# Emitting evictions and selection steps by modelled engine clocks, with two count chains, and FFN tiles in other pools

## The chip, the cores and the metric

The kernel runs on one core of one Trainium2 chip. The metric is the device time of one execution in microseconds (us). The core has TensorE (PE, matmuls; PEld is its weight load), VectorE (DVE), ScalarE (ACT), GpSimd (POOL) and SyncE (SP, which only issues DMAs). Each engine has a stream of instructions of its own, in the order in which the program holds them.

## The reference

One encoder layer on 2048 tokens of width 1024, in float32. Cut to what matters here:

```python
proj = x @ w_in                     # q, latent k/v, index q, index w, index k, pool input, two gates
rel = relu(einsum('bqhd,bsd->bqhs', q_idx, k_idx) * idx_scale)
idx_score = einsum('bqh,bqhs->bqs', w_idx * head_w_scale, rel)     # masked to admissible chunks
_, sel = top_k(idx_score, 256)      # each query attends to its 256 best keys
attn = softmax(q . k_lat[sel] * attn_scale) @ v_lat[sel]           # 8 heads, shared latent key/value
branch_a = (attn @ w_uv) @ w_attn_branch
branch_b = pool(pool_in) @ w_pool_branch       # trailing means over 2, 4, 8, 16 frames minus the frame
mixed = (sigmoid(gate_a) * branch_a + sigmoid(gate_b) * branch_b) @ w_out
x = layer_norm(ALPHA * x + mixed)
h = causal_conv3(x @ w_ffn_up); ffn = (silu(gate) * val) @ w_ffn_down
x = layer_norm(ALPHA * x + ffn)
```

## The kernel before

Every float32 product is made of three matmuls on a high and a low part (`mm3`); a part is made by a copy on ACT (`hi`) and a subtraction on DVE or POOL (`lo`). The stages follow one another: the index projections (`proj_index`, four token groups g of 512 tokens, to about 200 us), then for each g the pool projections, the query projections and the gates (`proj_pool`, `proj_q`, `proj_gates`, to about 1110 us), the attention (to about 1690 us), the mixing (`mix_out`, to about 1975 us), the FFN's up-projection in two halves (`up`, to about 2850 us) and its down-projection (`down`).

From `proj_pool` of g = 0 to the end of `proj_gates` of g = 3 the instructions are held in the order in which the Python program emits them, on every engine (`manual_schedule`, L827). The generators of the projections yield after every six matmuls, and `turn` (L379) is called at each yield. It puts in steps of a background generator (`bg`): the index scores of a token group (`index_scores`, L861) and then the selection of the 256 best keys (`select`, L935), for the groups (0, 1), 2 and 3 of `GROUPS` in turn. The selection is a search over 32 bits: each bit counts, for each block of 128 queries, how many scores reach a threshold tile `F`, and `decide` (two small DVE instructions) makes the next `F`. Half of the blocks are counted on DVE, the others on ACT (Sign with an accumulated output), which waits for `F` from DVE. After the bits a mask is made per block (ACT Sign, a scan and other steps on DVE) and stored (`msk`).

How much background `turn` puts in is ruled by a model: `Paced` adds a modelled cost to a clock of each engine (`Clocks`), and `turn` goes on while the slower of DVE and ACT is under `SLACK` = 3 us ahead of PE and a credit lasts, which grows with 0.75 of PE's modelled time. Some costs of the model are a PE matmul of n columns at 0.002 + n/2400 us, a fixed 0.05 us on ACT (0.28 with accumulated output), 0.07 us on DVE, and a scan at 1.04 ns an element.

The evictions of the projections' results from PSUM (four one-bank tiles `p1`) are emitted at fixed places: in `proj_q` (L677) an ACT copy right after the matmuls of each 128 tokens; after four of them `rope` on DVE rotates the rows, and `store_q` (L701) transposes earlier rows on PE and copies them out on ACT. The pool windows run on POOL in steps (`lazy_step`); one call after a window's last addition `less` (L758) emits, in one go, a DVE subtraction into `m`, the ACT copy of its high part, which reads `m`, and the DVE low part. The sigmoid gates are emitted two turns later (`after`).

`load_q` (L1054) needs the mask of block b and drains the background until it is emitted; `end_selection` (L304), called before the attention's block 8, drains all that is left.

In the FFN's up-projection (a held order as well, planned in `plan_up`, L1511, by due times around a period of 19.04 us for each of 44 quads of seven products) SBUF tiles of 4 KB a partition come from two pools: `T` (`big`, 34 tiles) and `L` (`more`, 12 tiles). Input combinations p = 1 and 2 (`x_load` L1437, `x_split` L1447) lie in `L`, the other five in `T`, four tiles each; the weights' parts (`up_hi`) and the convolution's sums (`conv_first`) lie in `T`, the raw weights in `L`.

Of the kernel before, what the change touches and what calls it, by code (L numbers as in the profile page):

```python
# [9 lines left out]
F32 = mybir.dt.float32  # L10
# [38 lines left out]
SLACK = 3.0  # L49
NPRE = 2  # L50
PN = (1, 1, 1)
PG = (0,)
HD, HP = 3, 5
# [5 lines left out]
DG = 2  # L59
DQ = 0  # L60
MS = 'vector'
FIN = 1
# [9 lines left out]
PAUSE = "pause"  # L72
GRAIN = 1
RATE = 0.75
CAP = 1.5
SCAN = 1.04
# [8 lines left out]
class Clocks:  # L85
# [7 lines left out]
    def slowest(self):  # L93
        return max(self.dve, self.act)

    def backlog(self):
        return self.slowest() - self.pe


class Paced:  # L100
# [5 lines left out]
    def __getattr__(self, name):  # L106
# [135 lines left out]
class Kern:  # L242
    def __init__(self, ctx, tc, a, out):
        self.clocks = Clocks()
        self.tc, self.nc, self.a, self.out = tc, PacedCore(tc.nc, self.clocks), a, out
        self.stores, self.older, self.bg, self.late = [], [], [], []
        self.const = ctx.enter_context(tc.tile_pool(name="const", bufs=1))
# [16 lines left out]
        self.credit = self.seen = 0.0  # L264
# [21 lines left out]
    def PS1(self, shape=(P, 512)):  # L286
        return self.p1.tile(list(shape), F32, tag="p1", name=self._name("p1_"))
# [16 lines left out]
    def end_selection(self):  # L304

        while self.bg:
            drain(self.bg.pop(0)[1])
# [70 lines left out]

    def turn(self, step=None):  # L379
# [8 lines left out]
        pe, work = self.clocks.pe, self.clocks.work  # L388
        self.credit = min(self.credit + RATE * (pe - self.seen), CAP)
        self.seen = pe  # L390
        while self.bg and self.clocks.backlog() < SLACK and self.credit > 0:
            ready, gen = self.bg[0]
            if not ready():
                break
            before = dict(work)
            step = next(gen, "end")
            if step == "end":
                self.bg.pop(0)
            if step == PAUSE:
                break  # L400
            self.credit -= max(work["dve"] - before["dve"], work["act"] - before["act"])
# [275 lines left out]
    def proj_q(self, g):  # L677
# [1197 lines left out]
```

## Time and profile before

| what | value |
|---|---|
| median of 3 runs | 3349.55 us (3349.07 to 3350.21) |
| the profiled execution | 3349.93 us, span of its instructions 3348.2 us |
| PE busy | 3203.2 us, 96% of the span |
| DVE, ACT, POOL busy | 2114.3, 1644.9, 1324.2 us |

A busy time is the time in which the engine had at least one instruction under way. The waits name what ended an idle stretch. [...] All operations are recorded through one helper, so every instruction has line 135, and tiles are told apart by name: `p` is PSUM, `b` a tile of `T`, `l` of `L`, `m` of the pool `mid`, `i` a row of scores, `F` and `h` the thresholds and their steps.

### The profile page before, as it was taken

How to read it: one execution, taken by the hardware profiler on the slowest of the kernel's cores; microseconds unless marked ns; L12 is line 12 of the kernel's file. 1: busy time of each engine (PE TensorE's matmuls, PEld its weight loads, DVE VectorE, ACT ScalarE, POOL GpSimd, SP SyncE). 2: the span in 40 equal slices, each digit the busy share in tenths (PEclk: the TensorE clock that was granted, in tenths of full speed). 3: DMA queues.
4: the chain of work that ended last, by engine and by line, in shares of the span. 5: the costliest groups of instructions: out<-in, count | busy, mean ns of one | idle time of the engine just before them, and what ended most of it. 6: DMA issues, size and time to landing. Idle time of an engine off the chain costs nothing. (4 is left out here: it accounts for less than half of the span.)

```text
span 3348.2 us, 45033 instructions
## 1 busy us (share of the span) xinstructions
PE 3203.2 (96%) x16198; PEld 2711.3 (81%) x16198; DVE 2114.3 (63%) x3724; ACT 1644.9 (49%) x2720; POOL 1324.2 (40%) x1283
## 2 busy tenths in 40 slices
PE   8899989989989799999999999999999999999998
PEld 8898878888878578888878878888778888888887
DVE  5567677876778787777755775565655455643543
ACT  3456636754667566666621134444544444433431
POOL 3148410010010432111221157777667777644552
PEclk9999999999989899999999999999999999999999
DMA  8368944735545211000164762332422222655552
GB/s 318 120 233 283 350 160 151 289 137 178 211 177 179 91 62 37 30 31 16 31 209 157 271 218 82 113 126 95 157 76 90 93 82 92 219 167 175 192 178 85
DMA packets 260142, 499.12 MB, mean 149 GB/s; under 512 B 19210, under 2 KB 136910, under 8 KB 259918
## 3 DMA queue, kind: packets, MB, share of 16 engines
q1 hardware_dynamic: 231182, 461.64, 39.8%
q10 hardware_dynamic: 28736, 34.61, 2.9%
q8 instruction: 127, 2.08, 0.3%
q14 instruction: 97, 0.79, 0.1%
HBM read 349.21 MB, written 146.96 MB: 148 GB/s over the span
## 5 line engine op out<-in xcount | busy, mean ns | idle before, releaser
L135 PE MATMUL p<-b,b 128*128 128x512 f32 (+3 forms) x12480 | 2642.0, 368 | 97.2 <-ACT b L135 45.0
L135 PEld LDWEIGHTS p<-b,b 128*128 128x128 f32 x12480 | 2147.3, 191 | 467.6 <-ACT b L135 51.5
L135 ACT ACTIVATE b<-p 128x512 fp32r<-128x512 f32 (+12 forms) x610 | 373.0, 632 | 351.4 <-PE p L135 337.0
L135 POOL TENSOR_TENSOR b<-b,b 128x256 fp32r<-128x256 f32 (+3 forms) x302 | 441.5, 1467 | 234.0 <-ACT b L135 196.4
L135 ACT ACTIVATE b<-i,F 128x1408 bf16<-128x1408 f32 (+4 forms) x224 | 322.1, 1438 | 154.3 <-DVE F L135 112.4
L135 ACT ACTIVATE b<-b 128x1024 fp32r<-128x1024 f32 (+2 forms) x264 | 231.7, 909 | 316.5 <-DMA b<-h 164.1
L135 PE MATMUL p<-l,b 128*128 128x512 f32 x1440 | 349.2, 397 | 1.6 <-DVE b L135 1.6
L135 POOL TENSOR_SCALAR b<-b 128x256 fp32r<-128x256 f32 (+3 forms) x214 | 113.5, 533 | 570.5 <-ACT b L135 287.1
L135 PEld LDWEIGHTS p<-l,b 128*128 128x128 f32 x1440 | 270.7, 188 | 66.6 <-DVE b L135 2.4
L135 DVE TENSOR_SCALAR_CACHE_REDUCE b<-i,F 128x1152 bf16<-128x1152 f32 (+7 forms) x238 | 314.8, 1323 | 3.6
L135 DVE TENSOR_TENSOR b<-b 128x512 fp32r<-128x512 f32 (+1 forms) x104 | 159.5, 1543 | 231.4 <-ACT b L135 227.8
L135 DVE TENSOR_TENSOR b<-p,b 128x512 fp32r<-128x512 f32 (+2 forms) x330 | 254.3, 780 | 62.5 <-ACT b L135 57.5
L135 POOL TENSOR_TENSOR b<-m,b 128x512 fp32r<-128x512 f32 x176 | 236.4, 1366 | 96.8 <-ACT b L135 94.2
L135 ACT ACTIVATE b<-m 128x512 fp32r<-128x512 f32 x224 | 136.2, 626 | 259.3 <-POOL m L135 166.4
L135 DVE TENSOR_TENSOR p<-p,m 128x512 f32<-128x512 f32 x132 | 91.8, 695 | 252.2 <-PE p L135 252.0
L135 ACT ACTIVATE b<-p,cw 128x1024 f32<-128x1024 f32 x88 | 106.3, 1208 | 282.9 <-DVE p L135 282.9
L135 PE MATMUL p<-ident,b 128*128 128x128 f32 x1456 | 215.0, 275 | 22.1 <-ACT b L135 12.2
L135 POOL TENSOR_TENSOR b<-l,b 128x512 fp32r<-128x512 f32 x132 | 173.8, 1332 | 135.2 <-ACT b L135 135.1
L135 DVE SCALAR_TENSOR_TENSOR b<-p,cw,b 128x1023 f32<-128x1023 f32 (+1 forms) x132 | 169.0, 1281 | 88.6 <-ACT b L135 54.9
L135 PEld LDWEIGHTS p<-ident,b 128*128 128x128 f32 x1456 | 175.0, 141 | 57.1 <-ACT b L135 15.7
L135 DVE CUSTOM_DVE_ANT_0 b<-p,b 128x1024 f32<-128x1024 f32 (+7 forms) x192 | 174.4, 909 | 68.3 <-PE p L135 67.7
L135 DVE SCALAR_TENSOR_TENSOR i<-b,ws,i 128x768 f32<-128x768 f32 (+9 forms) x154 | 154.8, 1027 | 59.5 <-ACT b L135 57.8
(136 smaller groups left out, 2224.3 us busy)
## 6 DMA issues: line engine op xcount, KB each, us to landing
b<-wp SPq DMA_DIRECT2D x192, 512.0 KB, 6.6
l<-in_w_ffn_up_dram SPq DMA_DIRECT2D x88, 512.0 KB, 5.1
b<-in_w_ffn_down_dram SPq DMA_DIRECT2D x88, 512.0 KB, 4.4
wp<-b SPq DMA_DIRECT2D x64, 512.0 KB, 6.6
h<-b SPq DMA_DIRECT2D x44, 512.0 KB, 2.7
b<-h SPq DMA_DIRECT2D x88, 256.0 KB, 3.9
b<-in_w_in_dram SPq DMA_DIRECT2D x32, 512.0 KB, 7.4
xT<-b SPq DMA_DIRECT2D x32, 512.0 KB, 6.9
```

Source lines behind the costliest of these rows:

```text
L135: return f(*args, **kw)
```

## The change

The costs of the clocks' model are set anew, the credit goes, and `SLACK` becomes 2.0 us, for each engine by itself. A heap of due steps is added: `evict` emits an eviction at the first turn at which the modelled PE clock is 0.25 us past its last matmul, and a following stage at the time at which the model has the earlier engine done. No more than two evictions (three in `pool_map`) stay open when a new `p1` tile is taken. The steps of `less`, of the scores and of the masks are cut apart in the same way. The background becomes a list of tasks, each bound to some engines; a task may yield a time until which it is held, or WAIT. In `select` the counts on ACT are a task of their own (`signs`), beside the counts on DVE, and each count there is held until the model has its threshold ready. In the FFN, `x` tiles p = 1 and 2 move from `L` to `T`, and the parts A11 and S2 and the convolution's sums from `T` to `L`. No arithmetic is changed. The diff, cut (the steps left out are cut apart in the same manner as those shown):

```diff
 LEAD = 2.5
-SLACK = 3.0
...
-SCAN = 1.04
+SCAN = 2.2
 PIECE = 256
...
             if self._w == "pe":
-                self._c.pe += 0.109 if name == "transpose" else 0.002 + max(n, 64) / 2400.0
+                self._c.pe += 0.109 if name == "transpose" else max(0.106, 0.0134 + n / 2400.0)
             else:
                 rate = {"dve": 1.04, "act": 0.84, "pool": 2.2}[self._w]
-                fixed = 0.07
-                if self._w == "act":
-                    fixed = 0.28 if "accum_out" in kw else 0.05
-                if self._w == "dve" and name in ("tensor_scalar", "tensor_copy") and "accum_out" not in kw:
+                fixed = 0.17
+                if "accum_out" in kw:
+                    fixed = 0.47 if self._w == "act" else 0.29
+                elif self._w == "dve" and name in ("tensor_scalar", "tensor_copy"):
...
-    def PS1(self, shape=(P, 512)):
+    def PS1(self, shape=(P, 512), ahead=2):
+        while len(self.open) > ahead:
+            self.evict_step(self.open[0], True)
         return self.p1.tile(list(shape), F32, tag="p1", name=self._name("p1_"))
...
-        while self.bg:
-            drain(self.bg.pop(0)[1])
+        self.force(lambda: not (self.tasks or self.bg))
...
 
+    def when(self, time, f):
+
+        self.serial += 1
+        heapq.heappush(self.due, (time, self.serial, f))
+
+    def run_due(self, until=None):
+        while self.due and self.due[0][0] <= (self.clocks.pe if until is None else until):
+            heapq.heappop(self.due)[2]()
+
+    def evict(self, *stages):
+
+        e = list(stages)
+        self.open.append(e)
+        self.when(self.clocks.pe + 0.25, lambda: self.evict_step(e))
+
+    def evict_step(self, e, all=False):
+        while e:
+            engine, f = e.pop(0)
+            f()
+            if e and not all:
+                self.when(getattr(self.clocks, engine), lambda: self.evict_step(e))
+                return
+        self.open = [o for o in self.open if o is not e]
+
     def turn(self, step=None):
         for t in self.late:
...
             self.older, self.stores = self.stores, []
-        pe, work = self.clocks.pe, self.clocks.work
-        self.credit = min(self.credit + RATE * (pe - self.seen), CAP)
-        self.seen = pe
-        while self.bg and self.clocks.backlog() < SLACK and self.credit > 0:
-            ready, gen = self.bg[0]
-            if not ready():
-                break
-            before = dict(work)
-            step = next(gen, "end")
-            if step == "end":
-                self.bg.pop(0)
-            if step == PAUSE:
-                break
-            self.credit -= max(work["dve"] - before["dve"], work["act"] - before["act"])
+        self.run_due()
+        self.background()
+
+    def spawn(self, gen, *engines):
+        task = {"gen": gen, "engines": engines, "hold": 0.0}
+        self.tasks.append(task)
+        return task
+
+    def next_group(self):
+
+        if not self.tasks and self.bg and self.bg[0][0]():
+            self.leader = self.spawn(self.bg.pop(0)[1], "act", "dve")
+        return bool(self.tasks)
+
+    def advance_task(self, t):
+        r = next(t["gen"], "end")
+        if r == "end":
+            self.tasks = [o for o in self.tasks if o is not t]
+        elif r == WAIT:
+            return False
+        elif r is not None:
+            t["hold"] = r
+        return True
+
+    def background(self):
+
+        moved = True
+        while moved and self.next_group():
+            moved = False
+            for t in list(self.tasks):
+                if t["hold"] <= self.clocks.pe and all(self.clocks.backlog(e) < SLACK for e in t["engines"]):
+                    moved |= self.advance_task(t)
+            self.run_due()
+
+    def force(self, done):
+
+        while not done() and self.next_group():
+            for t in list(self.tasks):
+                self.run_due(1e9)
+                self.advance_task(t)
...
+            def rotate(c=c, rows=rows):
+                v = rows.rearrange("p b (h d) -> p b h d", d=DL)
+                cs, sn = (t[:, bs, None, :].to_broadcast([P, RB, 2, ROT]) for t in (self.cos, self.sin))
+                halves = (v[:, :, :, 0:16], v[:, :, :, 16:32])
+                self.rope(halves, halves, cs, sn, [P, RB, 2, ROT])
+                self.qpend.append((g, c, rows))
+
             for rb in range(RB):
                 ps = self.PS1()
                 yield from self.proj_r(ps[:, :256], w, rb, 256)
-                self.after(DQ, lambda rb=rb, ps=ps, rows=rows:
-                           nc.scalar.activation(rows[:, rb], ps[:, :256], AF.Copy))
+                self.evict(("act", lambda rb=rb, ps=ps, rows=rows:
+                            nc.scalar.activation(rows[:, rb], ps[:, :256], AF.Copy)),
+                           *([("dve", rotate)] if rb + 1 == RB else []))
                 if rb:
                     self.lazy_step()
+                if rb == 1 and c > 1:
+                    self.store_q()
                 yield 2.6
-            self.flush()
-            v = rows.rearrange("p b (h d) -> p b h d", d=DL)
-            cs, sn = (t[:, bs, None, :].to_broadcast([P, RB, 2, ROT]) for t in (self.cos, self.sin))
-            halves = (v[:, :, :, 0:16], v[:, :, :, 16:32])
-            self.rope(halves, halves, cs, sn, [P, RB, 2, ROT])
-            self.qpend.append((g, c, rows))
-            if len(self.qpend) > 2:
-                self.store_q()
...
-            t = self.M([P, G])
-            self.nc.scalar.activation(t, ps, AF.Copy)
-            self.nc.scalar.dma_start(self.d_q[g][:, 2 * c + i], t)
+
+            def copy(i=i, ps=ps):
+                t = self.M([P, G])
+                self.nc.scalar.activation(t, ps, AF.Copy)
+                self.nc.scalar.dma_start(self.d_q[g][:, 2 * c + i], t)
+
+            self.evict(("act", copy))
...
-            self.fins.append([FIN, less])
+            self.when(self.clocks.pool, less)
...
-            t = self.T([P, 2, G], F32R)
-            self.split(t[:, 0], t[:, 1], p)
-            self.pooled.append(t)
+            self.when(max(self.clocks.dve, self.clocks.pool if g == 0 else 0), high)
+
+        def high():
+            t = st["t"] = self.T([P, 2, G], F32R)
+            nc.scalar.activation(t[:, 0], st["p"], AF.Copy)
+            self.when(self.clocks.act, low)
+
+        def low():
+            t = self.pooled[k] = st["t"]
+            nc.vector.tensor_tensor(t[:, 1], st["p"], t[:, 0].bitcast(F32), op=OP.subtract)
...
-                self.store_q()
...
                 w = self.ab.get(base + 2 * j + i)
                 ps = self.PS1()
                 yield from self.proj_t(ps, w)
+                if i == 0 and j < 2:
+                    self.store_q()
 
                 def gate(dst=self.d_gm[g][:, 2 * j + i, 0], ps=ps):
...
         for j in range(4):
...
+                    nc.vector.tensor_tensor(gates[i], ps, gates[i], op=OP.mult)
+                    self.store(self.d_gm[g][:, 2 * j + i, 1], gates[i])
+
+                self.evict(("dve", branch))
                 if j == 3 and g + 1 == NG:
                     self.scores_to(2 * i + 2)
...
+        def piece(row, wsc, h, lo, hi):
+
+            nch = 1 if hi - lo <= 512 else 2
+            cw = (hi - lo) // nch
+            ps = self.PS2([P, 2, 512])
+            for c in range(nch):
+                ks = slice(lo + c * cw, lo + c * cw + cw)
+                nc.tensor.matmul(ps[:, c, :cw], qh[:, h], self.kst[:, ks], start=True, stop=False)
+                nc.tensor.matmul(ps[:, c, :cw], ql[:, h], self.kst[:, ks], start=False, stop=True)
+
+            def relu():
+                rl = self.T([P, nch, cw])
+                nc.scalar.activation(rl, ps[:, :nch, :cw], AF.Relu, scale=ID ** -0.5)
+                st["used"] -= 1
+                self.when(self.clocks.act, lambda: add(rl.rearrange("p c w -> p (c w)")))
+
+            def add(rl):
+                if h == 0:
+                    nc.vector.tensor_scalar(row[:, lo:hi], rl, wsc, None, op0=OP.mult)
+                else:
+                    nc.vector.scalar_tensor_tensor(row[:, lo:hi], rl, wsc, row[:, lo:hi], op0=OP.mult, op1=OP.add)
+                st["left"] -= 1
+
+            st["used"] += 1
+            st["left"] += 1
+            self.when(self.clocks.pe + 0.25, relu)
...
+            while len(parts.get(b, ())) < 2:
+                yield WAIT
+            yield st["parts"]
...
+                for lo, hi in spans:
+                    while st["used"] > 1:
+                        yield WAIT
+                    piece(row, wsc, h, lo, hi)
                     yield
+            while st["left"]:
+                yield WAIT
...
+        ready = [0.0] * len(sets)
+
+        def settle(k, bit):
+            decide(k, bit, last[:, k - 1:k] if bit == 0 else None)
+            ready[k] = self.clocks.dve
+
+        def signs():
+            for bit in range(31, -1, -1):
+                for k in range(1, len(sets)):
+                    while ready[k] is None:
+                        yield WAIT
+                    yield ready[k]
+                    pend[k] = self.sml([P, 1], tag="ca", bufs=8)
+                    count(k, 0, pend[k])
+                    ready[k] = None
+                    self.when(self.clocks.act, lambda k=k, bit=bit: settle(k, bit))
+                    yield
+
+        last = self.sml([P, 4], I32, tag="F", bufs=10)
+        self.spawn(signs(), "act")
+        self.leader["engines"] = "dve",
         for bit in range(31, -1, -1):
             cd = self.sml([P, 4], tag="cd")[:, :len(sets[0])]
             for i in range(len(sets[0])):
                 count(0, i, cd)
-                if i + 1 < len(sets):
-                    if bit < 31:
-                        decide(i + 1, bit + 1)
-                    pend[i + 1] = self.sml([P, 1], tag="ca", bufs=8)
-                    count(i + 1, 0, pend[i + 1])
                 yield
             pend[0] = cd
             decide(0, bit)
-        f = self.sml([P, 4], I32, tag="F", bufs=10)
-        n = len(sets) - 1
-        for k in range(n):
-            decide(k + 1, 0, f[:, k:k + 1])
-        sets, F = [sets[0], [b for half in sets[1:] for b in half]], [F[0], f[:, :n]]
+        while len(self.tasks) > 1 or None in ready:
+            yield WAIT
+        self.leader["engines"] = "act", "dve"
...
+            yield self.clocks.dve
+            signed = []
+
+            def sign(i):
+                N = P * (half[i] + 1)
+                sg = self.T([P, N], F16)
+                nc.scalar.activation(sg, self.I[half[i]], AF.Sign, bias=tn[:, i:i + 1])
+                signed.append((sg, self.clocks.act))
+
+            sign(0)
             for i, b in enumerate(half):
                 N = P * (b + 1)
...
+                if i + 1 < nh:
+                    sign(i + 1)
+                sg, time = signed.pop(0)
+                yield time
+                eq, cu = self.T([P, N], F16), self.T([P, N], F16)
...
         else:
-            while self.selected < b:
-                if next(self.bg[0][1], "end") == "end":
-                    self.bg.pop(0)
+            self.force(lambda: self.selected >= b)
...
     def up_hi(self, q, name):
-        w = self.uparts[q, name] = self.T([P, 2, 4, P], F32R)
+        w = self.uparts[q, name] = (self.L if name in ("A11", "S2") else self.T)([P, 2, 4, P], F32R)
         self.nc.scalar.activation(w[:, 0], self.up_block(q, name), AF.Copy)
...
         for c in range(2):
-            t = (self.L if p in (1, 2) else self.T)([P, 2, G], F32R)
+            t = self.T([P, 2, G], F32R)
...
         for lo in self.xraw1.pop((hf, p)):
-            hi = (self.L if p in (1, 2) else self.T)([P, 2, G], F32R)
+            hi = self.T([P, 2, G], F32R)
...
         hf, n, v = self.conv_of(q, i)
-        a = self.ab[q, i] = self.T([P, 1024])
+        a = self.ab[q, i] = self.L([P, 1024])
```

## Rows read from the trace of the kernel before

**Rows 1.** The page's first part: busy time, share of the span, instructions of each engine.

```profile
span 3348.2 us, 45033 instructions
PE 3203.2 (96%) x16198; PEld 2711.3 (81%) x16198; DVE 2114.3 (63%) x3724; ACT 1644.9 (49%) x2720; POOL 1324.2 (40%) x1283
```

**Rows 2.** Windows: length, busy us of PE, PEld, DVE, ACT, POOL, granted clock, DMA share, GB/s.

```profile
100.00:200.00 100.00, 89.41 (x636) 84.24 (x635) 67.01 (x149) 54.03 (x100) 11.34 (x16) 0.98 0.30 104
200.00:1100.00 900.00, 852.47 (x4596) 743.02 (x4595) 668.41 (x1545) 557.92 (x809) 202.09 (x347) 0.98 0.62 220
440.00:480.00 40.00, 28.88 (x212) 27.59 (x212) 31.60 (x65) 10.54 (x20) 8.74 (x11) 0.87 0.35 121
480.00:690.00 210.00, 204.41 (x1083) 177.57 (x1083) 165.08 (x356) 145.96 (x206) 6.57 (x12) 1.00 0.56 201
950.00:1000.00 50.00, 36.33 (x238) 33.99 (x237) 36.67 (x82) 31.99 (x43) 5.25 (x6) 0.83 0.45 162
1100.00:1150.00 50.00, 26.06 (x119) 21.70 (x119) 38.71 (x110) 22.89 (x49) 14.23 (x23) 0.73 0.21 62
1150.00:1270.00 120.00, 112.35 (x649) 96.25 (x648) 98.65 (x211) 77.59 (x154) 48.88 (x43) 0.97 0.18 57
1270.00:1700.00 430.00, 427.31 (x2441) 361.94 (x2440) 306.10 (x612) 276.50 (x525) 82.54 (x79) 1.00 0.12 37
```

**Rows 3.** Waits: PE in 200:1100, then ACT in 440:480 and in 950:1000.

```profile
PE p L135 <- ACT b L135: 41.8, 25, 7.8
...
ACT b L135 <- DVE m L135: 9.4, 1, 9.4
...
ACT b L135 <- DVE h L135: 11.3, 4, 4.0
```

**Rows 4.** Timeline near 463 us: start, length, instruction, idle before and its end.

```profile
459.68 2.02 DVE L135 TENSOR_TENSOR_SCAN b<-b 128x896 f16<-128x896 f16 x1
...
462.78 0.63 ACT L135 ACTIVATE b<-m 128x512 fp32r<-128x512 f32 x1 [9.40 <-DVE m L135]
463.31 0.37 ACT L135 ACTIVATE b<-p 128x256 f32<-128x256 f32 x1
...
463.73 0.58 PE L135 MATMUL p<-b,b 128*128 128x256 f32 x1 [7.77 <-ACT b L135]
```

**Rows 5.** Timeline near 959 us.

```profile
957.04 2.00 ACT L135 ACTIVATE b<-i,F 128x2048 bf16<-128x2048 f32 x1 [3.97 <-DVE h L135]
...
957.26 1.95 DVE L135 TENSOR_SCALAR_CACHE_REDUCE b<-i,F 128x1664 bf16<-128x1664 f32 x1
...
959.46 0.74 PE L135 MATMUL p<-b,b 128*128 128x256 f32 x4 [3.14 <-ACT b L135]
```

**Rows 6.** The score rows' tile i in 890:1120: min/median/max ns, first and last start.

```profile
L135 DVE TENSOR_SCALAR_CACHE_REDUCE b<-i,F x68: 1931/2068/2340, 893.6 to 1118.9; 128x1664 bf16<-128x1664 f32 x33, 128x1792 bf16<-128x1792 f32 x33, 128x1920 bf16<-128x1920 f32 x1, 128x2048 bf16<-128x2048 f32 x1
...
L135 ACT ACTIVATION_READ_ACCUMULATOR b<-i,F x64: 185/187/202, 893.5 to 1110.8; 128x1 f32 x64
...
  DVE F L135: 39.4, 27
  DVE h L135: 18.1, 12
```

**Rows 7.** Timeline, end of the projections and start of the attention.

```profile
1112.46 0.69 PE L135 MATMUL p<-b,b 128*128 128x128 f32 x2 [8.84 <-ACT b L135]
...
1115.42 1.22 DVE L135 TENSOR_TENSOR b<-b,b 128x1024 fp32r<-128x1024 f32 x1
...
1116.69 1.12 PE L135 MATMUL p<-b,b 128*128 128x128 f32 x4 [3.55 <-DVE b L135]
...
1145.11 4.70 PE L135 MATMUL p<-b,b 128*128 128x256 f32 x18 [8.26 <-DVE nd L135]
```

**Rows 8.** Windows before and in the first half of the FFN's up-projection.

```profile
1974.00:2000.00 26.00, 20.81 (x98) 16.27 (x98) 22.22 (x17) 15.39 (x20) 23.08 (x22) 0.96 0.77 268
2000.00:2400.00 400.00, 400.00 (x1741) 328.06 (x1741) 222.35 (x225) 177.64 (x315) 297.52 (x230) 0.99 0.32 108
```

**Rows 9.** DVE's timeline at the FFN's start and at the change of its halves.

```profile
1994.49 3.91 DVE L135 TENSOR_TENSOR b<-b,b 128x1024 fp32r<-128x1024 f32 x2
...
2405.68 8.40 DVE L135 TENSOR_TENSOR l<-l,l 128x1024 fp32r<-128x1024 f32 x4
```

More of the change, by code (lines that the diff above doesn't have):

```diff
@@ L48 @@
 LEAD = 2.5
-SLACK = 3.0
+SLACK = 2.0
 NPRE = 2
-PN = (1, 1, 1)
-PG = (0,)
-HD, HP = 3, 5
+HD, HP = 2, 4
 XAT = 0
@@ L91, in __init__, with backlog @@
         self.shared = False
[L93 to L97, printed above, removed]
+    def backlog(self, engine):
+        return getattr(self, engine) - self.pe
 class Paced:
@@ L798, in proj_gates @@
             if j == 3:
+                while len(self.pooled) < 4:
+                    self.run_due(self.due[0][0])
                 yield from self.pool_map(g)
-            if self.qpend and j < 2:
-                self.store_q()
-            while self.lazy or j and self.fins:
+            while self.lazy:
                 self.lazy_step()
@@ L812, in gate @@
                     nc.scalar.dma_start(dst, ga)
-                self.after(DG, gate)
+                self.evict(("act", gate))
                 yield 5.2
@@ L836, in gate @@
                     gates.append(gb)
-                self.after(DG, gate)
+                self.evict(("act", gate))
                 yield 5.2
@@ L879, in prepare, with high, low @@
                 nc.tensor.transpose(ps[:, h], qd[:, h].rearrange("p a d -> p (a d)"), self.ident)
-            parts[b] = self.split_new(ps)
+            def high():
+                hi = parts[b] = [self.T(list(ps.shape), F32R)]
+                nc.scalar.activation(hi[0], ps, AF.Copy)
+                self.when(self.clocks.act, low)
+            def low():
+                lo = self.T(list(ps.shape), F32R)
+                nc.vector.tensor_tensor(lo, ps, parts[b][0].bitcast(F32), op=OP.subtract)
+                parts[b].append(lo)
+                st["used"] -= 1
+                st["parts"] = self.clocks.dve
+            st["used"] += 1
+            self.when(self.clocks.pe + 0.25, high)
+        def piece(row, wsc, h, lo, hi):
[9 more added lines that the diff above has]
+                nc.scalar.activation(rl, ps[:, :nch, :cw], AF.Relu, scale=ID ** -0.5)
+                st["used"] -= 1
+                self.when(self.clocks.act, lambda: add(rl.rearrange("p c w -> p (c w)")))
[5 more added lines that the diff above has]
+                st["left"] -= 1
+            st["used"] += 1
+            st["left"] += 1
+            self.when(self.clocks.pe + 0.25, relu)
+        st = {"used": 0, "left": 0, "parts": 0.0}
         load(blocks[0])
-        for _ in range(PN[0] if g in PG else 1):
-            yield PAUSE
+        yield self.clocks.pe + 10.0
         double(blocks[0])
-        for _ in range(PN[1] if g in PG else 1):
-            yield PAUSE
+        yield self.clocks.dve
         prepare(blocks[0])
-        for _ in range(PN[2] if g in PG else 1):
-            yield PAUSE
         for b in blocks:
@@ L898, in index_scores @@
             row = self.place(b)
-            tiles = [row[:, lo:hi] for lo, hi in spans]
             for h in range(IH):
@@ L903, in index_scores @@
                 if h == HP and more:
+                    while st["used"] > 1:
+                        yield WAIT
                     prepare(b + 1)
                 wsc = self.ws[:, b, h:h + 1]
[L906 to L920 removed]
+                for lo, hi in spans:
+                    while st["used"] > 1:
+                        yield WAIT
+                    piece(row, wsc, h, lo, hi)
                     yield
+            while st["left"]:
+                yield WAIT
             getattr(nc, MS).memset(row[0:64, N - 64:N], NEG)
@@ L985, in select @@
             decide(0, bit)
-        f = self.sml([P, 4], I32, tag="F", bufs=10)
-        n = len(sets) - 1
-        for k in range(n):
-            decide(k + 1, 0, f[:, k:k + 1])
-        sets, F = [sets[0], [b for half in sets[1:] for b in half]], [F[0], f[:, :n]]
+        while len(self.tasks) > 1 or None in ready:
+            yield WAIT
+        self.leader["engines"] = "act", "dve"
+        sets, F = [sets[0], [b for half in sets[1:] for b in half]], [F[0], last[:, :len(sets) - 1]]
         for k, half in enumerate(sets):
```

55 lines of the change are left out of this document (15 added, 40 removed).

## The prediction

> **What bounds the kernel now.** I read the page first: PE is busy 3203.2 of 3348.2 us, no other engine over 63% [rows 1]. So no matmul time is to be had from this change, only the 145.0 us in which PE is idle and what its clock loses. The windows say where: PE is idle 100 - 89.4 = 10.6 us in 100:200, 900 - 852.5 = 47.5 in 200:1100, 23.9 in 1100:1150 and 7.7 in 1150:1270, together 89.7 us [rows 2]. In the next 430 us, the attention without background, it is idle 2.7. The granted clock is below full speed in the same windows and nearly nowhere else before the mixing. I price that as (1 - clock) times busy: 0.02 x 89.4 = 1.8, 0.02 x 852.5 = 17.0, 0.27 x 26.1 = 7.0, 0.03 x 112.4 = 3.4, together 29.2 us, with about 4 us of rounding in the second. What this change can win in the projections and just behind them is thus at most 89.7 + 29.2 = 118.9 us.
>
> The waits then name who keeps PE waiting: in 200:1100 it is ACT for 41.8 us in 25 stops [rows 3]. But ACT is busy only 62% there [rows 2], so the question is what ACT itself was waiting for: in 440:480 a tile m of DVE for 9.4 us at once, in 950:1000 threshold steps h of DVE for 11.3 us [rows 3]. Two stretches of the timeline show the whole mechanism. Near 463 us DVE is in a scan of 2.02 us; ACT stands 9.40 us before a copy that reads m, which DVE makes behind such scans; the eviction of a PSUM tile (0.37 us) stands behind that copy; PE stands 7.77 us until it is through [rows 4]. Near 959 us a count on ACT stands 3.97 us until DVE has the threshold, takes 2.00 us, and only then comes the eviction that PE has been waiting for, 3.14 us [rows 5]. In both cases the work is short and the order is what costs: a waiting instruction at the head of ACT's order, the eviction behind it. Four one-bank PSUM tiles are all the reserve that PE has.
>
> **The change, part by part.**
>
> *The held order.* An eviction is now emitted when the model has the matmuls done, and the copy that reads m, the counts on ACT and the relus when the model has DVE or PE done. If the clocks are near the truth, ACT no longer stands before an empty input with an eviction behind it. What stands ahead of an eviction is then at most the 2.0 us of `SLACK` plus one instruction begun under it, 2.0 + 0.19 us for the longest count with its accumulator [rows 5, 6]: 4.2 us. PE meanwhile has three other PSUM tiles; 24 matmuls of 256 columns at the model's 0.12 us are 2.9 us a tile, so some 8.6 us. The reserve holds, less at the transposes of `store_q`, which take two tiles close together.
>
> Are the clocks near the truth? The new costs give 0.47 + 2048 x 0.00084 = 2.19 us for that count, shown 2.00 + 0.19; 0.29 + 1664 x 0.00104 = 2.02 for a DVE count, shown 1.95 before its accumulator; 0.17 + 896 x 0.0022 = 2.14 for the scan that took 2.02, which the old costs had at 1.0 [rows 4 to 6]. For PE, 1741 matmuls in 400.0 us of the FFN are 0.230 us each [rows 8]; the new cost of 512 columns is 0.2267, the old one 0.2153. So the new model is right to a few per cent where the old one hid half of every scan.
>
> I therefore take most of 200:1100 as won. What stays I take from stretches with the same mix and no pile-up: 480:690 keeps 5.6 us of 210 (2.7%), the pure attention 2.7 of 430 (0.6%) [rows 2]. Nearer to the second, 1.1% of 900, is 10 us idle; of the clock's 17.0 us I leave 3. Term: -(37.5 + 14) = -51.5 us, bounds -32 (2.7% stay, and half of the clock's share) and -64.5 (nothing stays).
>
> In 100:200 the order isn't held, and the evictions are emitted as before; only the background's steps are paced anew. I take half of 10.6 + 1.8, -6, bounds 0 and -12.
>
> [...]
>
> *1100 to 1270.* Here the attention starts while the last selection still runs. PE's first score matmul waits 8.84 us for the copy of q, then 3.55 for its low part, 1.22 us of DVE work behind a count, and later 8.26 us behind a mask's scan [rows 7]. With at most 2 us ahead on either engine the first two become about 2 us plus the copy and 2 + 1.2, less what overlaps; the chain from score to maximum of the small first blocks is data and stays. I leave 9 of 23.9 us idle and 2.5 of 7.0 for the clock: -19.5, bounds 0 and -31.
>
> In 1150:1270 all depends on whether the selection is over. Its last 32 bits took 1118.9 - 893.6 = 225 us, 7.0 us a bit, while ACT's two counts are 4.3 us and DVE's 4.0, and ACT sat idle 39.4 + 18.1 us for F and h [rows 5, 6]: the two chains have room once each goes at its own pace, and the credit that held back DVE is gone. What is left for DVE after 1100: it is busy 38.7 + 98.7 = 137.4 us to 1270, of which attention's own share, 306.1/427.3 of PE's 138.4 busy us, is 99; 38 us remain [rows 2]. To do them earlier, DVE must be busy (668 + 38) / 852 = 83% in place of 74%. The best stretches show 79 and 82%. I take half of 7.7 + 3.4: -5.5, bounds 0 and -11.
>
> Instructions added: none. The store_q transposes move by a few matmuls, with their copies and the two ACT-queue stores each; the masks' stores leave as before at a turn.
>
> *The FFN's tiles.* By the plan's due times `T` holds 20 x tiles, at most 6 weight parts and 4 convolution sums, 30 of 34, and `L` 8 + 4, all 12. After it `T` holds 28 + 5 = 33 and `L` 4 + 2 + 4 = 10. In 2000:2400 PE is busy all the time [rows 8], so nothing can be won there, and with one tile free little should be lost. At the border of mixing and FFN, x for p = 1 and 2 now competes for `T` with 8 tiles of `mixed`, 8 of the output weights, 4 rows and 2 norm vectors; the splits of p = 2 and 3 (two DVE steps each, 3.91 us a pair) move past the last mixing matmul, onto a DVE that is busy 22.2 of 26 us [rows 8, 9]. Between a gain of the 5.2 us that PE is idle there and a loss of both pairs, 7.8, I take +4, as DVE has little room. At the change of halves the pile of subtractions (8.40 us for four) [rows 9] keeps its due times: 0.
>
> Sum: -51.5 - 6 - 19.5 - 5.5 + 4 = -78.5 us against the profiled execution's 3349.9 (span 3348.2 and 1.7 around it), which is 0.4 above the median: 3271 us.
>
> **The rivals.**
>
> *Late selection.* If holding every threshold until the next turn makes a bit longer than 7.0 us, the selection isn't done when the attention reaches its block 8, and `force` emits the rest in one go with PE behind it. For it: the turns are six matmuls apart, and each bit on ACT now takes two of them. Against: the 57.5 us for which ACT sat idle. The wins behind 1100 (25 us) are lost and up to the 38 us of DVE work stand bare: 3296 to 3334, say 3315.
>
> *All of it.* No stop remains and the selection ends early: 3349.9 - 118.9 = 3231, with small remains up to 3250.
>
> *The clock stays low.* Many short waits take the place of few long ones. Against: 480:690 had 5.6 us of such waits at a granted clock of 1.00 [rows 2]. The forecast's clock gain, 14 + 0.9 + 4.5 + 1.7 = 21 us, would be lost: 3292. [...]
>
> [...]
>
> *The other side: the FFN starves.* With 33 of 34 tiles taken, a weight part's copy on ACT gets a tile only when PE ends the product before it, and PE then waits for that part. Price: at most one product, 19.04/7 = 2.7 us, in each of 44 quads, 119 us: 3390. It outweighs the rest from 78.5/44 = 1.8 us a quad. Against: the parts are due about 8 us or more ahead of their products, and `L` ran with all 12 taken while PE lost nothing [rows 8].
>
> **How the numbers follow.** Forecast 0.58 (its own range 3250 to 3300), late selection 0.14, all of it 0.08, clock low 0.07, clocks off 0.05, FFN starved 0.08. Half of "all of it" lies below 3243; that, clocks off and the FFN are left out, 0.17: 3243 to 3335. The runs of before spread by 0.03%; 0.2%, 6.7 us, is what I take as told from no change. Faster 0.58 + 0.14 + 0.08 + 0.07 = 0.87, same 0.05, slower 0.08.
>
> **What would show it.** In the windows after: PE idle in 200:1100 about 10 us (now 47.5) at a clock of 0.99 or 1.00; PE's waits for ACT there under 12 us; no ACT idle of several us on m, F or h right ahead of an eviction; the bits of the last selection under 6.5 us each and its masks stored by about 1150, with DVE near 83%; 9 us idle around the attention's start; a border of mixing and FFN that costs a few us more; 400.0 busy in 400 us of the FFN. The prediction is wrong if the last mask leaves after the attention's block 8, or if ACT's idle time on DVE stays where it was.

## The result, and the profile after

The change makes the kernel slower: 3371.07 us median (3368.40 to 3373.11, four runs) against 3349.88 for the kernel before on the same chip, a ratio of 1.0062 with a 95% interval of 1.0045 to 1.0080. The forecast was 3271 us, its range 3243 to 3335.

The page of the profiled execution (3370.73 us), its first part and the group of ACT's counts, then that group of before. The last columns are idle time ahead of the group and what ended most of it.

```profile
span 3369.0 us, 44939 instructions
PE 3207.6 (95%) x16198; PEld 2699.4 (80%) x16198; DVE 2113.3 (63%) x3724; ACT 1644.5 (49%) x2720; POOL 1347.4 (40%) x1283
...
L126 ACT ACTIVATE b<-i,F 128x1408 bf16<-128x1408 f32 (+4 forms) x224 | 321.8, 1437 | 38.9 <-DVE h L126 13.7
```

```profile
L135 ACT ACTIVATE b<-i,F 128x1408 bf16<-128x1408 f32 (+4 forms) x224 | 322.1, 1438 | 154.3 <-DVE F L135 112.4
```

The work is the same; ACT's idle time ahead of its counts has gone from 154.3 to 38.9 us. The windows of after, for the stretches of [rows 2]:

```profile
100.00:200.00 100.00, 99.31 (x712) 92.03 (x711) 46.65 (x138) 34.79 (x86) 41.76 (x71) 1.00 0.72 242
200.00:1100.00 900.00, 870.61 (x4687) 746.57 (x4686) 657.21 (x1508) 547.56 (x832) 224.66 (x327) 0.99 0.59 208
440.00:480.00 40.00, 40.00 (x227) 35.02 (x226) 33.67 (x132) 26.42 (x50) 0.30 (x3) 1.00 0.57 200
480.00:690.00 210.00, 204.58 (x1158) 177.74 (x1157) 153.31 (x294) 112.38 (x165) 13.93 (x18) 1.00 0.55 196
950.00:1000.00 50.00, 48.08 (x205) 38.11 (x206) 43.10 (x71) 37.43 (x42) 0.00 (x0) 1.00 0.63 216
1100.00:1150.00 50.00, 42.15 (x241) 35.59 (x241) 47.11 (x112) 41.87 (x73) 18.11 (x19) 0.96 0.15 46
1150.00:1270.00 120.00, 84.48 (x461) 69.02 (x459) 114.33 (x240) 84.65 (x128) 23.44 (x23) 0.91 0.09 28
1270.00:1700.00 430.00, 395.42 (x2249) 334.90 (x2250) 311.30 (x615) 270.69 (x504) 74.68 (x72) 0.95 0.10 32
```

In the projections the change does what it says. PE is busy 9.9 us longer in 100:200 and 18.1 longer in 200:1100, though this stretch now holds 46 us of the attention. Of the stretches of the pile-ups, 440:480 is full and 950:1000 is busy 48.08 of 50 us. Then PE is idle 35.5 us in 1150:1270, where before it was idle 7.7, and 34.6 in 1270:1700, where before it was idle 2.7. DVE is busy 114.33 of the 120 us of 1150:1270.

I cut the run at the attention's first and last score step on DVE: 1118.7 and 1658.0 us before, 1054.3 and 1675.5 after. So the attention starts 64.4 us earlier, takes 81.9 us longer (621.2 in place of 539.3), and what follows takes 3.3 longer (1693.5 in place of 1690.2): together +20.8, the difference of the spans. The two windows so cut, of before and then of after:

```profile
100.00:1118.69 1018.69, 947.29 (x5250) 831.33 (x5248) 752.62 (x1719) 618.56 (x915) 222.69 (x379) 0.97 0.58 206
1118.69:1657.98 539.29, 520.76 (x2959) 442.98 (x2960) 401.19 (x871) 350.11 (x684) 126.61 (x122) 0.98 0.11 35
```

```profile
100.00:1054.32 954.32, 935.83 (x5240) 811.31 (x5238) 672.20 (x1523) 545.01 (x837) 249.03 (x377) 1.00 0.62 219
1054.32:1675.53 621.21, 532.41 (x2961) 447.05 (x2961) 488.43 (x1061) 419.81 (x758) 124.00 (x129) 0.93 0.10 32
```

The question is those 81.9 us. PE is idle for 88.8 us of the attention (621.21 - 532.41), before 18.5: that is 70.3 of them. The other 11.6 are longer busy time, at a granted clock (the share of its full speed that TensorE had on average in a window) of 0.93 in place of 0.98. The waits of after, PE in 200:1100, then PE in 1050:1350 (us in all, times, longest):

```profile
PE p L126 <- ACT b L126: 16.9, 58, 2.8
...
PE p L126 <- DVE mx L126: 63.7, 11, 44.0
PE p L126 <- DVE b L126: 20.6, 11, 3.4
```

Where PE waited for ACT 41.8 us in 25 stops [rows 3], it now waits 16.9 us in 58, none over 2.8. The price comes in the attention, where PE waits for DVE: for mx, the row maximum that DVE makes of each score tile, and for b, here mostly the low parts that DVE makes of the transposed tiles. DVE's counts in the attention, after and then before:

```profile
L126 DVE TENSOR_SCALAR_CACHE_REDUCE b<-i,F 128x1664 bf16<-128x1664 f32 (+3 forms) x40 | 80.8, 2021 | 0.3
```

```profile
L135 DVE TENSOR_SCALAR_CACHE_REDUCE b<-i,F 128x1920 bf16<-128x1920 f32 (+1 forms) x2 | 4.5, 2272 | 0.0
```

Of the selection's counts on DVE 80.8 us stand in the attention, where before had 4.5. One stop shows how a count gets in the way. It stands ahead of a low part of DVE, and PE's next transposes wait 3.41 us for that:

```profile
1131.72 2.07 DVE L126 TENSOR_SCALAR_CACHE_REDUCE b<-i,F 128x1792 bf16<-128x1792 f32 x1
...
1133.72 0.68 DVE L126 TENSOR_TENSOR b<-p,b 128x512 fp32r<-128x512 f32 x1
...
1134.55 0.74 PE L126 MATMUL p<-ident,b 128*128 128x128 f32 x4 [3.41 <-DVE b L126]
```

The score rows' tile i (min/median/max ns, first and last start) says how far the last search was, first up to the attention's start, then from there to 1250:

```profile
L126 DVE TENSOR_SCALAR_CACHE_REDUCE b<-i,F x28: 1876/2008/2080, 968.1 to 1050.4; 128x1664 bf16<-128x1664 f32 x14, 128x1792 bf16<-128x1792 f32 x14
...
L126 DVE TENSOR_SCALAR_CACHE_REDUCE b<-i,F x35: 1915/1948/2079, 1075.3 to 1249.1; 128x1664 bf16<-128x1664 f32 x18, 128x1792 bf16<-128x1792 f32 x17
```

Two counts are a bit. 14 of the 32 bits are made when the attention starts, at 6.1 us each (82.3 us for 27 counts), under the 7.0 of [rows 6] (6.9 by the 64 counts on ACT, since the 225 us there hold four counts for the masks too); in the attention a bit takes 10.2 us (173.8 for 34). At block 8 the first row of more than 1024 columns needs the memory of the score rows, `end_selection` forces what is left, and PE stands (start, length, idle before):

```profile
1249.65 0.94 PE L126 MATMUL p<-b,b 128*128 128x512 f32 x3
1294.61 3.36 PE L126 MATMUL p<-b,b 128*128 128x512 f32 x7 [44.01 <-DVE mx L126]
```

The masks, the last of which left at 1271.7 us before, leave between 1269.7 and 1305.9. Up to the attention the search itself is quicker; it starts late. The score matmuls of after, for groups 0 and 1, 2, and 3 (first and last start):

```profile
L126 PE MATMUL p<-kst,b x160: 306/363/500, 137.7 to 283.8; 128*128 128x384 f32 x48, 128*128 128x512 f32 x48, 128*128 128x320 f32 x32, 128*128 128x448 f32 x32
...
L126 PE MATMUL p<-kst,b x256: 289/322/449, 535.8 to 616.5; 128*128 128x288 f32 x32, 128*128 128x320 f32 x32, 128*128 128x352 f32 x32, 128*128 128x384 f32 x32
...
L126 PE MATMUL p<-kst,b x256: 344/378/503, 860.6 to 964.8; 128*128 128x416 f32 x32, 128*128 128x448 f32 x32, 128*128 128x480 f32 x32, 128*128 128x512 f32 x32
```

Before they run 113.5 to 201.3, 476.5 to 565.6 and 778.9 to 890.4 us. So the first scores end 82 us later, the last 74, while the projections that cover all this end 64 us sooner.

### The profile page after: what moved, and what is told of

Same layout as the page of the kernel before. It is cut to its first block, busy times and chain, and to the rows that moved or that the text cites. A ratio compares the mean times of both kernels' runs of the same rounds, so it can differ in the third digit from the quotient of the medians.

```text
span 3369.0 us, 44939 instructions
## 1 busy us (share of the span) xinstructions
PE 3207.6 (95%) x16198; PEld 2699.4 (80%) x16198; DVE 2113.3 (63%) x3724; ACT 1644.5 (49%) x2720; POOL 1347.4 (40%) x1283
## 5 line engine op out<-in xcount | busy, mean ns | idle before, releaser
L126 ACT ACTIVATE b<-b 128x512 fp32r<-128x512 f32 (+1 forms) x228 | 193.6, 885 | 327.6 <-DMA b<-h 161.8
L126 ACT ACTIVATE b<-i,F 128x1408 bf16<-128x1408 f32 (+4 forms) x224 | 321.8, 1437 | 38.9 <-DVE h L126 13.7
L126 PE MATMUL p<-b,l 128*128 128x512 f32 x1056 | 253.1, 395 | 0.0
L126 DVE TENSOR_TENSOR b<-p,b 128x512 fp32r<-128x512 f32 (+1 forms) x286 | 202.0, 713 | 70.2 <-ACT b L126 62.1
L126 PEld LDWEIGHTS p<-b,l 128*128 128x128 f32 x1056 | 199.0, 189 | 46.4
L126 ACT ACTIVATE l<-p,cw 128x1024 f32<-128x1024 f32 x88 | 106.3, 1208 | 250.6 <-DVE p L126 250.6
L126 DVE SCALAR_TENSOR_TENSOR l<-p,cw,l 128x1023 f32<-128x1023 f32 (+1 forms) x132 | 169.1, 1281 | 88.8 <-ACT l L126 53.9
L126 POOL TENSOR_TENSOR b<-m,b 128x512 fp32r<-128x512 f32 x132 | 173.7, 1331 | 112.2 <-ACT b L126 112.2
L126 ACT ACTIVATE b<-b,mx 128x1024 f32<-128x1024 f32 (+7 forms) x192 | 171.5, 896 | 59.4 <-DVE mx L126 56.0
L126 ACT ACTIVATE b<-m 128x512 fp32r<-128x512 f32 x180 | 112.5, 625 | 172.5 <-DVE m L126 84.8
```

The source lines that it names most:

```text
L126: return f(*args, **kw)
```

## The experiments

Theory L, the late selection: the change wins in the projections, and loses because DVE does too little of the selection before the attention. Rival A: the new order slows the attention itself. Rival B: what is left over can't be hidden in the attention at all, wherever its end is forced. Rival F: the FFN's tiles cost. All runs but e4 and e9 are single executions; the kernel before, seven times beside them, spread from 3347.3 to 3354.3 us, so a few us between two times tell nothing.

**e1 and e2: the last search cut.** Group 3's search ends after 12 of its 32 bits (its masks are coarser than the reference's).

```diff
-for bit in range(31, -1, -1):
+for bit in range(31, end - 1, -1):    # end = 20 if blocks[0] >= 12 else 0
```

e1 (after):

> The changed kernel, but the search for token group 3 stops after 12 of its 32 bits (20 bits of counts left out, so its masks are coarser). Theory 1, the late selection: the whole loss comes from the search of group 3 that is still under way when the attention starts, so the time falls by the drain at block 8 and the slow attention before it, to 3265 to 3295 us, and PE idle in the attention's first 250 us falls from about 100 us to under 25. Rival, the attention or the FFN is slower for another reason (tiles, order): the time stays above 3340 us, less at most the 20 us that the counts themselves keep DVE busy beside PE.

e2 (before):

> The kernel before, with the same 20 bits left out: what the bits cost there. Theory 1: they run beside PE, apart from the waits near 960 to 995 us and at the attention's start, so 3305 to 3335 us, and the changed kernel without them beats it by 30 us or more. Rival: both kernels lose about the same with the bits, and stay about 20 us apart with the changed one slower.

Measured: 3302.24 and 3303.64 us. None of the four forecasts was met: theory 1 had e1 at 3295 at most and the kernels 30 us apart, the rivals had e1 above 3340 and the kernels 20 apart. The 21 us between the kernels are gone, but nothing is won: in e1 the attention starts 34.4 us sooner than in e2 (1064.5, 1098.9) and takes 28.9 longer (542.3, 513.4). Its last masks still left between 1163 and 1238 us and 27 us more of DVE's work than in e2 lie in its attention, so this didn't tell L from A.

**e5 and e6: all three searches cut**, `end = 20` for every group.

e5 (after):

> The kernel after, with the search of all three selections cut to 12 of 32 bits (the thresholds, and so the masks, are coarser than the reference's). Theory L (the change loses only because the selection is late): no selection work is left in the attention, so the attention starts at about 1040 us, takes the 513 us that it took in the kernel before with few bits (1098.9 to 1612.3) and 1690 from there to the end: 3245 to 3265 us, no bare stretch around 1250. Rival A (the new order of evictions itself slows the attention's first blocks): attention start to last score still takes 540 us, as in the run with few bits for group 3 alone: 3285 to 3300.

e6 (before):

> The kernel before, with the same bits left out of all three selections. Theory L: the pile-ups on ACT stay per bit but there are fewer bits; the held order is still 25 to 35 us slower than the changed one to the attention's start: 3275 to 3295, 20 to 40 us behind the changed kernel with the same bits. Rival A: the two come out within 10 us of each other.

Measured: 3272.48 and 3306.21 us. The windows of e5, up to the attention and in it:

```profile
100.00:1064.49 964.49, 938.33 (x5241) 814.21 (x5239) 567.02 (x1082) 420.61 (x636) 255.16 (x381) 1.00 0.62 219
1064.49:1578.48 513.99, 512.12 (x2961) 437.01 (x2961) 368.41 (x824) 342.28 (x679) 122.23 (x125) 1.00 0.11 35
```

With no mask left to make, the attention takes 514.0 us in the new order and 513.3 in the old: A falls. The start is 34.2 us sooner (1098.7 in e6). My 1040 for it was 24 us too early, and both times lie 7 to 11 us above what I had expected.

**e3: without the dear prices.** The model charges DVE 1.6 times the rate and 0.25 us more while `shared` is set, in group 0.

```diff
-                self.clocks.shared = g == 0
```

> The changed kernel without the dearer DVE prices that the clocks use for token group 0 (1.6 times the rate and 0.25 us more). Theory 1a, the background falls behind first in group 0, where the dear prices fill the modelled DVE while the real one is about 60% busy: all phases of the selection come 30 to 50 us earlier, about 6 to 9 bits fewer are left for the attention, and the time falls to 3310 to 3345 us. Rival 1b, the delay is made by the holds at the start of each group and by ACT's chain: the phases come less than 15 us earlier and the time stays above 3355 us. If the prices were needed, new PE waits of some us appear between 200 and 300 us.

Measured: 3349.41 us, 21.7 under after, between the two ranges. The first scores end at 229 us in place of 284, the last at 911 in place of 965; 443 us of DVE's work lie in the attention in place of 488. The prices did protect something: PE is busy 141.82 of the 150 us of 300:450, in after 149.21.

**e4: the FFN's tiles moved back** to the pools of before, all else as after.

> The changed kernel with the FFN's tiles in the pools of the kernel before. If the moved tiles cost what I forecast (4 us) the time falls to 3367 us; if they are neutral it stays within 2 us of 3371; if they gained at the change of halves (PE idle 13.4 us there before, less after), it rises to 3375 to 3380 us.

Measured: 3370.39 us (3368.46 to 3374.55), 1.0068 of before, 1.0051 to 1.0084: F falls as the cause of the 21 us. The runs' spread leaves room for the few us that I had forecast.

**e7: the forced end at block 10.**

```diff
-            if npc == 2 and self.spare is None:
+            if b >= 10 and self.spare is None:
-    s = self.spare.tile(...) if pc else self.T([P, n])
+    s = self.spare.tile(...) if pc and self.spare else self.T([P, n])
```

> The kernel after, with the forced end of the selection moved from the attention's block 8 to its block 10: the second halves of the score rows of blocks 8 and 9 take tiles of the pool T, so that the selection's rows may stay two blocks longer. Theory L: DVE is already saturated there, so two blocks more hide a part of the 57 us that stand bare, some 20 to 40 us; the rest stands bare at block 10: 3330 to 3355. Rival B (the work is only moved, since the attention's own DVE work leaves no room for it): 3365 to 3375; if T runs short, slower still.

Measured: 3371.37 us, as after. PE's timeline has the stop at 1350 now:

```profile
1349.60 0.95 PE L126 MATMUL p<-b,b 128*128 128x512 f32 x3
1369.53 2.93 PE L126 MATMUL p<-b,b 128*128 128x512 f32 x6 [18.98 <-DVE mx L126]
```

The first stop is 19 us in place of 44, but PE, busy 38.66 of 50 us in 1250:1300, loses the rest on the way, and the attention takes 621.3 us, as after. L's expectation, that two more blocks hide 20 to 40 us, was wrong; B holds, and L has to be put with it: what isn't done before the attention is paid in it.

**e8 and e9: the selection made earlier**, in four edits that leave the clocked order alone.

```diff
-                self.clocks.shared = g == 0
-        yield self.clocks.pe + 10.0
+        yield self.clocks.pe + 5.0
-        for g in groups:
-            yield from self.index_scores(g)
+        yield from self.index_scores(blocks)          # groups 0 and 1 as one list
-        while len(self.tasks) > 1 or None in ready:   # before any mask
-            yield WAIT
+            while k and (len(self.tasks) > 1 or None in ready):   # k = 1: the masks of ACT's blocks
+                yield WAIT
```

e8:

> The kernel after, with the selection made earlier and nothing else: the dear prices of group 0 are not used, groups 0 and 1 are scored as one list of blocks, the hold after the first load is 5 us in place of 10, and the masks of the blocks whose counts DVE makes are made without waiting for ACT's counts. Theory L: the last masks are stored at about the attention's block 8, the bare stretch is under 15 us, and DVE has room in the attention: 3270 to 3300, faster than both kernels. Rival A: 3330 or more, since the attention's first blocks stay slow under the new order.

e9, timed:

> The kernel of e8 again, timed in rounds. Theory L: 3303 us as there, 45 to 50 us under the kernel before: a ratio of 0.985 to 0.988. Rival (e8's one execution was a lucky one): within 0.2% of before.

Measured: 3303.14 us, and timed 3301.96 (3298.22 to 3307.67) against 3351.28: a ratio of 0.9856, 0.9840 to 0.9873. It beats both kernels; e8's own range ended 3 us lower. Its last mask leaves at 1239.7 us, and PE has no stop there (busy 49.81 of 50 us in 1250:1300). e8's windows:

```profile
100.00:1081.45 981.45, 943.89 (x5241) 816.32 (x5239) 787.15 (x1750) 624.83 (x916) 224.54 (x374) 0.99 0.60 214
1081.45:1607.50 526.05, 517.36 (x2959) 438.81 (x2960) 384.35 (x838) 346.18 (x682) 127.02 (x132) 0.99 0.11 36
```

Beside the same two windows of after, e8 puts 115 us more of DVE's work ahead of the attention, pays 27 us for it there, and gets 95 back.

**e10: e8 with the dear prices kept.** Its diff is e8's without the first line.

> The kernel of e8, but with the dear prices of group 0 kept as in the kernel after. Theory L, which says that each part of the lead counts by how much of the last selection it brings forward: about half of it is lost, the last masks come behind a forced stretch at block 8 again, 25 to 40 us bare: 3330 to 3350. Rival (the prices protect group 0's projections and pay for themselves): 3295 to 3308.

Measured: 3338.0 us. Of the 68 us between after and e8 the prices are thus 35 and the other three edits 33 if the prices are taken out last; taken out first (e3) they are 22, and the others 46. The two act in different places. With the prices kept, e10's first scores end at 198 us (before 201, after 284), and DVE is as busy in 100:200 as in e8 (71.99):

```profile
100.00:200.00 100.00, 96.75 (x671) 88.64 (x670) 71.06 (x169) 55.88 (x106) 9.05 (x16) 0.98 0.35 122
```

So in these first 100 us it is mostly the hold and the two lists of blocks that cost; which of the two wasn't tried. The prices cost in 200:300, where DVE is busy 54.38 us in e10 and 86.31 in e8, and protect in 300:450, where PE is busy 150.00 of 150 us in e10 and 135.88 in e8. Prices in between weren't tried.

**e11: the kernel before, its last selection begun later.**

```diff
+        for _ in range(12 if g == 3 else 0):
+            yield PAUSE
         load(blocks[0])
```

> The kernel before, with its last selection begun 12 turns (about 35 us) later and nothing else. Theory L: in the old order too, lateness is paid in full behind the attention's block 8, since DVE has little room in the attention: 3370 to 3390, and its last masks come from a forced stretch. Rival (the old order has room, the changed one lost through its own steps): 3345 to 3358.

Measured: 3371.84 us. The old order becomes as slow as the changed kernel when its last counts begin at 917 us in place of 892: the start is unmoved (1117.3), the attention takes 24.1 us more for the 25 us of delay.

```profile
100.00:1117.29 1017.29, 946.98 (x5242) 831.02 (x5241) 727.59 (x1673) 604.40 (x901) 223.41 (x379) 0.97 0.58 206
1117.29:1680.65 563.36, 528.87 (x2962) 447.75 (x2962) 426.46 (x916) 363.29 (x698) 123.75 (x122) 0.96 0.11 35
```

**e12: e8 with ACT's counts and their thresholds off the clocks.**

```diff
-                    while ready[k] is None:
-                        yield WAIT
-                    yield ready[k]
...
-                    ready[k] = None
-                    self.when(self.clocks.act, lambda k=k, bit=bit: settle(k, bit))
+                    settle(k, bit)
```

> The kernel of e8, but with the counts on ACT and the thresholds made from them on DVE emitted without looking at the clocks, one chain behind the other's back, while the evictions stay clocked. If the counts' waits made the old pile-ups: ACT stands before F for several us at a time again and PE waits for ACT more than the 9.7 us of e8 in 200:1050, by 15 us or more: 3315 to 3335. If the evictions' clocks alone did it: 3295 to 3308.

Measured: 3322.99 us, 20 us lost, 17.7 of it ahead of the attention (start 1099.2, length 525.9): there PE is idle 10.4 us longer, and its work takes 7.3 longer at a granted clock of 0.98 in place of 0.99. PE's waits in 200:1050, e8 and then e12:

```profile
PE p L126 <- DVE b L126: 10.0, 3, 6.8
PE p L126 <- ACT b L126: 9.7, 43, 1.2
...
PE p L126 <- ACT m L126: 3.5, 1, 3.5
```

```profile
PE p L126 <- DVE b L126: 16.2, 4, 9.6
PE p L126 <- ACT b L126: 11.9, 46, 0.8
PE p L126 <- ACT m L126: 7.9, 3, 4.1
```

The time fits the first expectation and its mechanism doesn't: ACT's part grows by 6.6 us, not by 15, and DVE's by as much, in stops of up to 9.6. So the clocks of the counts are worth 17.7 (1099.2 - 1081.5) of the 37.2 us by which e8 starts its attention before the old kernel. How the evictions share in the rest wasn't tried.

All runs side by side, from the windows cut at each run's own first and last score:

| run | attention starts | DVE busy, 100 to start | attention takes | DVE busy in it |
|---|---|---|---|---|
| e2, before, few bits | 1098.9 | 691.6 | 513.4 | 368.3 |
| e6, before, few bits in all | 1098.7 | 560.3 | 513.3 | 368.1 |
| e5, after, few bits in all | 1064.5 | 567.0 | 514.0 | 368.4 |
| e8 | 1081.5 | 787.2 | 526.1 | 384.4 |
| e12 | 1099.2 | 783.9 | 525.9 | 384.4 |
| e1, after, few bits | 1064.5 | 676.8 | 542.3 | 395.8 |
| before | 1118.7 | 752.6 | 539.3 | 401.2 |
| e11, before, late | 1117.3 | 727.6 | 563.4 | 426.5 |
| e3 | 1073.9 | 723.7 | 583.0 | 443.2 |
| e10 | 1062.1 | 716.1 | 584.7 | 444.1 |
| e7 | 1056.4 | 671.0 | 621.3 | 487.1 |
| after | 1054.3 | 672.2 | 621.2 | 488.4 |

The fourth column follows the last, in either order: over e2, each us of DVE's work beyond 368 costs 0.78 us (e12) to 1.05 (e1), and 107.8/120.1 = 0.90 in after. ACT's counts are moved along with DVE's (419.8 us of ACT's work lie in the attention of after, 343.5 in e2's), and no run moves DVE's alone; but in e8, e1 and before ACT has at most 7 us more than in e2, and the price is 0.79 to 1.05 there already. The change moved 488.4 - 401.2 = 87.2 us of DVE's work into the attention; at 0.90 that is 78 of the 81.9 us. L stands, with B in it.

## Why the prediction was wrong

*The held order* (-51.5) *and 100:200* (-6): right in mechanism, too large. The start came 64.4 us sooner, but with 80 us less of DVE's work done ahead of it. Where that work is cut in both kernels the start comes 34.2 us sooner (e5, e6), and where it is done, with 35 us more than before, 37.2 (e8). PE is idle 15.6 us in 200:1050, where before it was 47.5 and I left about 10 to 1100. The waits for ACT fell to 16.9 us, above the 12 I had named. The clock came back as taken: 0.99 in 200:1100, 1.00 in 440:480 and 950:1000. Nor did many short waits keep it low: 58 stops of at most 2.8 us for ACT stand in 200:1100, at a granted clock of 0.99.

*1100 to 1270* (-19.5 and -5.5): here the prediction failed, at the step "To do them earlier, DVE must be busy (668 + 38) / 852 = 83% in place of 74%", and in taking half of the 11 us behind that as won, with 0 as the worst bound. I asked how much selection was left in the trace of before and moved it forward, as if what is left could only shrink. The 38 were about right for before (401.2 - 368.3 = 33). But the head start itself takes time from the selection, and DVE's pace didn't rise: it was busy 621.8 of 850 us in 200:1050 (73%; before 626.7), and 46.7 in 100:200 (before 67.0). Of the 80 us that after does less ahead of the attention, 20 are thus missing in the first 100 us (the holds and lists of e10), 5 up to 1050, and 55 behind it, where before still had 69 us of projections and after 4. So not 38 but 488.4 - 368.3 = 120 us were left, and in place of a gain of 25 us behind 1100 the attention took 81.9 longer. Nearly the 83% were to be had: e8 is busy 690.8 of 850 us there, 81%, and wins. The sign that I had named for a wrong prediction came too: the last mask left behind the forced end at block 8, at 1305.9 us.

*The rival "late selection"* had the outcome and the place (`force` at block 8), but not the cause: its condition, bits longer than 7.0 us, didn't come about, since ahead of the attention a bit takes 6.1 us. Its price was capped at those 38 us, its chance at 0.14. I held the 57.5 us of ACT's idle time against it. Much of that time did come back, but the starts of the scores, which the diff's holds, waits and prices push back, decide more than the pace, and I had no term for them.

*Clocks off* (0.05, no change in the time): ACT's stops didn't come back, 16.9 us in 200:1100 where before had 41.8. A DVE step did run longer beside POOL's work: near 2908 us of before a low part of 512 columns takes 2.86 us beside a POOL step of 2.39, near 2913, begun ahead of one, 0.69.

*The FFN* (+4, and the rival of 3390): no starving, and no cost that the runs could tell. In e4 the median is that of after within 0.7 us, in runs that spread by 5 and 6 us, and with the FFN shifted by its 19 us PE is busy 360.00 of 360 us in 2039:2399.

## What to carry to other kernels

When a change shortens a stretch that also carries background work for a later one, work out how much of that work still fits: the lead that is won is taken from the background. Price what is left over by what the next stage waits for, not by the idle share of the engine that has to do it. And look at when each background step may first start, not only at its pace: here four small edits to holds, waits and prices turned a loss of 0.6% into a gain of 1.4%.

## What the hardware showed

In the pure attention (e2) DVE is busy 368.3 of 513.4 us, 72%, and still has little room: each us of other work cost 0.78 to 1.05 us in these runs, 0.90 in after. The waits say how it passes on: in the attention of after PE waits 63.7 us for mx, 53.2 of them in the forced stretch, mostly before its next scores, and 18.6 for b, mostly before its next transposes. DVE makes both in its program's order, behind the counts of 2 us that stand ahead of them, as near 1134 us. That all of the 0.90 us comes this way is argued, not shown. And this standstill is paid at the clock too: after the 44.01 us PE's first seven matmuls of 512 columns start 0.45 us apart (1294.6 to 1297.3), twice the 0.23 us of the FFN [rows 8]; in 1250:1300 the granted clock is 0.54, in 1255:1305 0.50.
